# S5 parameters, tables and early weight splits moved to VectorE, complex products over both parts at once, new chain delays

## The chip, the cores and the metric

One NeuronCore of a Trainium2 chip runs the whole program. The metric is the device time of one execution in microseconds (us), the median over several runs. Names of engines in the rows: PE is TensorE's matmul, PEld its weight load, DVE VectorE, ACT ScalarE, POOL GpSimd, SP the engine that issues most DMAs. SBUF is the on-chip memory of 128 partitions, PSUM the banks that matmuls write.

## What is computed

One layer over 1024 prompt positions and 32 new ones, model width 1024. One projection of RMSNorm(x) gives q, k, v, an attention gate ga, the S5 input u and an S5 gate gs, each 512 wide. The attention branch is stick-breaking attention (8 heads of 64). The S5 branch is a complex diagonal state space model with 32 groups of 16 channels and 64 complex states each:

```python
dt = jnp.exp(log_dt)[:, None]; mag = jnp.exp(a_re * dt); ang = a_im * dt
ab_re, ab_im = mag * jnp.cos(ang), mag * jnp.sin(ang)
# f = (ab - 1) / a ; bb = f * b ; bu = ug @ bb
_, _, h_re, h_im = lax.associative_scan(_cmul_combine, (a_s_re, a_s_im, bu_re, bu_im), axis=0)
y = einsum(h_re, c_re) - einsum(h_im, c_im) + d_skip * u
y = gelu(y); y = y * sigmoid(y @ w_glu + b_glu)
out = concat[rmsnorm(att) * silu(ga), rmsnorm(y) * silu(gs)] @ w_out
```

The result is x + out, normed, besides k, v and the last states.

## The kernel before

Every fp32 product runs as three matmuls on a high and a low part of each operand. So weights are split: ScalarE copies w_raw to w_hi, then w_lo = w_raw − w_hi (`w_split`, `w01_split`); x is split the same way (`x_split`: xh on ScalarE, xl on VectorE). `x_sq` squares the rows of x on ScalarE and sums them on VectorE; `x_rs` turns the sum into the factor rsx with matmuls by ones, `rsqrt` on GpSimd and a broadcast by matmul.

`proj_first` (L378 is its matmul) computes the first two projections u0 and u1 while x arrives. Then `proj` (L353) goes through u2, u3, gs0 to gs3, ga0, q0, k0 and v0, each in three pieces of 256, 384 and 416 columns with eight **steps** of three matmuls. After every step `tick` lets the S5 tasks (generators) issue what is due: a task yields a number of steps or the name of something that must be done. So the program order on every engine is fixed when the kernel is built, by the steps at which tasks are started and by the delays in the table WAIT. Each engine then runs its own queue in order.

The S5 work is cut into four groups m of eight channel groups. The parameter chain `params_a` (exp, angle reduction) runs on GpSimd. `angles` makes the rotation table RT by ScalarE's sine, `params_b` to `params_d` the powers PW of the transition and bb. For each m:

- `s_tables` forms three tables by complex products: W (PW times bb, on VectorE), rot (RT far times near, on GpSimd) and V (PW times cv, on GpSimd, for m = 2 on VectorE). A complex product is `cms`: six operations, each over one of the two parts, 512 columns wide.
- `s_mats` transposes W on TensorE (L763), forms Ms (L770, L772) and sends it through DRAM to the tile Tm.
- `u_evac`/`u_raw`, `u_store` and `u_load` move the projection u through DRAM (uj, ud, U).
- `s_states` multiplies U by WT (L873), rotates the result b by rot into E, scans E along time (L891), rotates back into b (named bst in the rows). I call its end S0 to S3.
- `s_out` adds U·Tm (L920) and bst·V (L926), applies GELU, and brings y through DRAM (yd, yj) to y_nat.

After y of group 3, `open_glu` loads the GLU weights, `glu` multiplies (L1033), `ssm_gate` gates with gs on VectorE and GpSimd and ends with `sums`. The attention part, woven with the remaining projections and the output product, follows. `act`, `tt` and `ts` are the helpers that most operations stand under, L96, L99 and L101 to L105.

Of the kernel before, what the change touches and what calls it, by code (L numbers as in the profile page):

```python
# [11 lines left out]
I32 = mybir.dt.int32  # L12
# [15 lines left out]
RSS = 47  # L28
# [40 lines left out]
def hymba_step(ctx, tc, xT, xn, w_in, ln_g, kcT, vc, w_glu, b_glu, w_out, g_att, g_ssm, final_g,  # L69
# [204 lines left out]
    for k in range(1, KT):  # L274
# [91 lines left out]
    def proj_first(evacs, banks):  # L366
# [3 lines left out]
        for c, k in [(0, k) for k in range(LEAD)] + [(c, k - LEAD * c) for k in range(LEAD, KT) for c in range(2)] + \  # L370
# [5 lines left out]
            for n_, (i, f) in enumerate(mms):  # L376
# [7 lines left out]
                if c and k == KT - 1 and f < 2:  # L384
                    w_split(4 + f)
# [1490 lines left out]
```

## Time and profile before

| | |
|---|---|
| runs | 726.07 us median of 3 (725.12 to 727.79) |
| the profiled execution | 723.47 us, span 721.7 us |
| TensorE matmul busy | 638.7 us, 88% of the span |
| VectorE | 505.8 us, 70% |
| GpSimd | 353.4 us, 49% |
| ScalarE | 344.8 us, 48% |
| mean granted TensorE clock | 0.937 of 2.4 GHz |

Busy shares are means over the span, and say little about one stretch; the granted clock is 1.00 or 0.50 at a time. A row of waits names the operation that waited and the one that released it. Matmul durations overlap, so the distance from start to start tells their pace.

### The profile page before, as it was taken

To read this page: it belongs to the slowest core of one execution; us is meant where nothing else is said; L and a number is where in the kernel's file an instruction comes from. 1 tells how busy PE (TensorE), PEld (TensorE's weight loads), DVE (VectorE), ACT (ScalarE), POOL (GpSimd) and SP (SyncE) were. 2 spreads that over 40 slices of the span, in tenths; PEclk is the share of its full clock that TensorE was granted. 3 is DMA by queue.
4 is the path that set the end of the run, shared out by engine and by line. 5 is a ranking of instruction groups with operands and counts; after the bars stand their busy time and mean duration, and the time that the engine had idled before them with its cause. 6 is when DMAs were issued, how large, how long until landed. Compare 5 with 4: busy or idle time off the path is not lost.

```text
span 721.7 us, 10881 instructions
## 1 busy us (share of the span) xinstructions
PE 638.7 (88%) x3834; PEld 574.6 (80%) x3834; DVE 505.8 (70%) x681; ACT 344.8 (48%) x753; POOL 353.4 (49%) x519
## 2 busy tenths in 40 slices
PE   8947987889999998999899999888998789889995
PEld 7947776787898998889889899787878567777883
DVE  5628699988524457678778686867777878695554
ACT  7521221141235464566756557555666647542332
POOL 4875896656222336743344433524135423233785
PEclk8969596989999999999999999999999899999998
DMA  8202522442351136210122112222135465347652
GB/s 306 67 15 67 140 59 73 143 156 71 122 166 60 40 108 216 80 42 23 60 77 75 43 30 82 89 68 94 35 113 165 142 215 165 118 149 214 216 186 94
DMA packets 62645, 79.14 MB, mean 110 GB/s; under 512 B 8864, under 2 KB 47072, under 8 KB 62592
## 3 DMA queue, kind: packets, MB, share of 16 engines
q1 hardware_dynamic: 56256, 66.93, 29.2%
q10 hardware_dynamic: 6336, 11.54, 5.0%
q8 instruction: 30, 0.49, 0.3%
q14 instruction: 23, 0.19, 0.1%
HBM read 51.97 MB, written 26.48 MB: 109 GB/s over the span
## 4 chain that ended last, share of the span: by engine, by line
PE 32%; DVE 19%; ACT 8%; POOL 8%; issue 7%; DMA 3%; ACTq 0%; DVEq 0%; POOLq 0%; SPq 0%
PE pj L353 12%; DVE cb L1169 5%; PE pj L1587 5%; DVE wtl L99 3%; PE z L1033 3%; PE pv L1231 2%; PE tr L1268 2%; PE z L1124 2%; ACT wth L96 2%; DVE kv_out L99 2%; POOL betaL L99 1%; DMA w_raw<-in_w_in 1%; POOL rst L105 1%; ACT cb L96 1%; ACT kA L96 1%
## 5 line engine op out<-in xcount | busy, mean ns | idle before, releaser
L353 PE MATMUL pj<-xh,w_hi 128*128 128x256 f32 (+2 forms) x456 | 160.2, 351 | 0.8 <-DVE kv_out L99 0.8
L353 PE MATMUL pj<-xl,w_hi 128*128 128x256 f32 (+2 forms) x456 | 148.9, 327 | 0.0
L353 PE MATMUL pj<-xh,w_lo 128*128 128x256 f32 (+2 forms) x456 | 148.7, 326 | 0.0
L1169 DVE TENSOR_TENSOR_SCAN cb<-cb 128x896 f32<-128x896 f32 (+8 forms) x66 | 98.9, 1505 | 5.5 <-ACT cb L96 5.4
L99 POOL TENSOR_TENSOR w_lo<-w_raw,w_hi 128x512 fp32r<-128x512 f32 x44 | 68.8, 1564 | 67.8 <-ACT w_hi L96 67.7
L353 PEld LDWEIGHTS pj<-xh,w_hi 128*128 128x128 f32 x456 | 88.8, 195 | 5.8 <-issue 2.6
L353 PEld LDWEIGHTS pj<-xl,w_hi 128*128 128x128 f32 x456 | 88.5, 194 | 1.5
L353 PEld LDWEIGHTS pj<-xh,w_lo 128*128 128x128 f32 x456 | 87.7, 192 | 0.3
L99 POOL TENSOR_TENSOR betaL<-betaL,cb 128x896 f32<-128x896 f32 (+2 forms) x24 | 44.2, 1842 | 70.2 <-DVE cb L1169 36.4
L99 DVE TENSOR_TENSOR wtl<-tr,wth 128x512 fp32r<-128x512 f32 (+2 forms) x86 | 53.5, 625 | 28.2 <-ACT wth L96 27.5
L96 ACT ACTIVATE cb<-z 128x512 f32<-128x512 f32 (+4 forms) x102 | 49.7, 487 | 45.0 <-DVE betaL L99 13.7
L1587 PE MATMUL pj<-xh,S 128*128 128x512 f32 (+3 forms) x212 | 69.2, 406 | 0.5 <-ACT w_raw L96 0.5
L99 POOL TENSOR_TENSOR betaS<-betaS,cb 128x128 f32<-128x128 f32 (+3 forms) x32 | 27.9, 879 | 74.6 <-DVE cb L1169 56.2
L96 ACT ACTIVATE wth<-tr 128x512 fp32r<-128x512 f32 (+2 forms) x86 | 47.3, 551 | 8.8 <-PE tr L1268 6.0
L1231 PE MATMUL pv<-wth,vS 128*128 128x256 f32 x160 | 43.5, 293 | 2.6 <-POOL wth L1208 2.6
L1587 PE MATMUL pj<-xl,S 128*128 128x512 f32 (+3 forms) x112 | 43.8, 393 | 0.7 <-DVE xl L99 0.7
L1268 PE MATMUL tr<-ident,betaL 128*128 128x128 f32 x208 | 33.9, 281 | 11.8 <-DVE wtl L99 9.0
L1587 PEld LDWEIGHTS pj<-xh,S 128*128 128x128 f32 (+2 forms) x212 | 37.9, 192 | 7.5 <-ACT w_raw L96 0.8
L1231 PE MATMUL pv<-wtl,vS 128*128 128x256 f32 x160 | 41.8, 284 | 0.4 <-DVE wtl L99 0.4
L99 DVE TENSOR_TENSOR kv_out<-pj,rsx 128x256 f32<-128x256 f32 (+2 forms) x55 | 28.1, 512 | 17.8 <-PE pj L353 16.8
L1268 PEld LDWEIGHTS tr<-ident,betaL 128*128 128x128 f32 x208 | 25.0, 143 | 17.0 <-DVE wtl L99 10.9
L96 ACT ACTIVATE betaL<-z 128x512 f32<-128x512 f32 (+4 forms) x70 | 35.9, 513 | 0.0
(337 smaller groups left out, 1600.5 us busy)
## 6 DMA issues: line engine op xcount, KB each, us to landing
w_raw<-in_w_in ACTq DMA_DIRECT2D x44, 256.0 KB, 2.6
x<-in_xn SPq DMA_DIRECT2D x8, 512.0 KB, 5.3
yp_d<-x SPq DMA_DIRECT2D x8, 512.0 KB, 5.5
x<-yp_d SPq DMA_DIRECT2D x8, 512.0 KB, 4.5
y_out<-x SPq DMA_DIRECT2D x8, 512.0 KB, 2.9
xr<-in_xT SPq DMA_DIRECT2D x7, 528.0 KB, 7.3
wraw<-in_w_out SPq DMA_DIRECT2D x5, 512.0 KB, 5.1
ud<-uj SPq DMA_DIRECT2D x4, 532.0 KB, 5.8
```

Source lines behind the costliest of these rows:

```text
L96: nc.scalar.activation(out, in_, f, **kw)
L99: (eng or nc.vector).tensor_tensor(out, a, b, op)
L105: (eng or nc.vector).tensor_scalar(out, a, s1, s2, o1, o2)
L353: nc.tensor.matmul(ps[:, :n], a[:, k], b[:, k, t0:t0 + n], start=(k == 0 and f == 0), stop=(k == KT - 1 and f == 2))
L1033: nc.tensor.matmul(ps[:, :n], a[:, k, m * 128:(m + 1) * 128], b[:, k, :n], start=(k == 0 and f == 0), stop=(k == 3 and f == 2))
L1124: nc.tensor.matmul(ps[:, :nn], a, b, start=(i == 0), stop=(i == len(mms) - 1 and mask is None))
L1169: nc.vector.tensor_tensor_scan(cc[:, ::-1], cc[:, ::-1], cc[:, ::-1], 1.0, OP.mult, OP.bypass)
L1231: nc.tensor.matmul(st["ps"][:, 0:256], vs[:, kb, 128 * h:128 * h + 128], w[:, c0:c0 + 256], start=(st["n"] == 0), stop=(st["n"] == 2 * nbl ...
L1268: nc.tensor.transpose(pp[:, c0:c0 + 128], b[:, 128 * kb:128 * kb + 128], ident)
L1587: nc.tensor.matmul(ps[:a.shape[1], :m], a, b_, start=(k == 0 and f == 0), stop=(k == 3 and f == len(mms) - 1))
```

## The change

The parameter chain moves to VectorE, is written with fused operations (a scalar operation and a tensor operation in one), and is placed between the splits of x, by ("p", n) in the list PREP and by `some`; its input pin is loaded from ScalarE's queue. Of the sums of squares the first three go to GpSimd. The low part of the weights of u2 to ga0 is formed on VectorE (WDVE 1 to 8 and the `w_split` in `proj_first`), that of the later ones stays on GpSimd. PW's powers, rot and V come from GpSimd to VectorE, and a complex product is done over both parts at once: `cmw` and `cmr` need wide operations (1024 columns and more) on repeated or negated copies (Pm, Bm, FT, NR) that ScalarE makes. The small copies into rot and fin go from GpSimd to ScalarE. The start steps RSS and PST and the table WAIT have new numbers.

```diff
-RSS = 47
+RSS = 52
...
-PST = 44
+PST = 45
...
-WDVE = 1
-RD = ()
-VD = (2,)
+WDVE = 8
...
-WAIT = {'md': (0, 0, 4, 2), 'Tm': (10, 14, 7, 8), 'ud': (1, 1, 2, 5), ... 'y': (17, 10, 16, 14), 'gate': (10, 10, 10, 11)}
+WAIT = {'md': (0, 0, 6, 0), 'Tm': (11, 14, 6, 0), 'ud': (1, 1, 0, 4), ... 'y': (17, 10, 16, 20), 'gate': (9, 9, 7, 8)}
...
     def x_sq(k):
         act(xr[k], xr[k], AF.Square)
-        if k in SQP:
+        if 0 < k < 4:
             tt(xr[0], xr[0], xr[k], OP.add, nc.gpsimd)
-        elif k > SQD:
-            tt(xr[SQD], xr[SQD], xr[k], OP.add)
+        elif k > 4:
+            tt(xr[4], xr[4], xr[k], OP.add)
+        if k == 7:
+            tt(xr[0], xr[0], xr[4], OP.add)
...
+        stt(t2, t1, -0.693359375, x, OP.mult, OP.add)
...
+        for i in range(6, 0, -1):
+            stt(out, out, 1.0 / math.factorial(i), t2, OP.add, OP.mult)
+            yield
...
+    nc.scalar.dma_start(pin, prm)
...
     x_split(0, first[0])
+    some(7)
     x_split(0, first[1])
+    some(5)
...
-                    w_split(4 + f)
+                    w_split(4 + f, nc.vector)
...
+        def cmw(out, a, s, b, t):
+            n = out.shape[1] // 2
+            tt(t, s, b[:, n:3 * n], OP.mult)
+            yield
+            tt(out, a, b[:, 0:2 * n], OP.mult)
+            yield
+            tt(out, out, t, OP.add)
+            yield
+
+        def cmr(out, a, b, t, conj=False):
+            r = [a[:, i:i + 1].to_broadcast(list(b.shape)) for i in range(2)]
+            tt(t, r[1], b[:, ::-1], OP.mult)
+            yield
+            tt(out, r[0], b, OP.mult)
+            yield
+            for i in range(2):
+                tt(out[:, i], out[:, i], t[:, i], OP.add if conj == (i == 0) else OP.subtract)
+                yield
...
-                   PW[:, 0, :, 1:s + 1], PW[:, 1, :, 1:s + 1], br, bi, t9[:, :, :s], gp)
+                   PW[:, 0, :, 1:s + 1], PW[:, 1, :, 1:s + 1], br, bi, t9[:, :, :s])
...
+            Pm = ss.tile([128, 5, 4, 9], F32, name="Pm")
+            act(Pm[:, 0:2], PW[:, 0:1, g].to_broadcast([128, 2, 4, 9]))
+            act(Pm[:, 2], PW[:, 1, g], scale=-1.0)
...
-            for _ in cms(W[:, 0], W[:, 1], pr, pi, xr_, xi_, t):
+            for _ in cmw(W.rearrange("p r q j c -> p (r q) j c"), two(Pm, 0, slice(0, 8)),
+                         two(Pm, 2, slice(0, 8)), three(Bm), t):
...
-            for _ in cms(ro[0], ro[1], far[0], far[1], near[0], near[1], tv, None if m in RD else gp):
+            for r, f in ((0, FT[:, 2]), (1, RT[:, 1, g, 16:24])):
+                tt(t[:, 4 * r:4 * r + 4], f[..., None].to_broadcast(s4),
+                   RT[:, 1 - r, g, None, 0:16].to_broadcast(s4), OP.mult)
                 yield 1
-            gp.tensor_copy(rot[:, :, :, 128], RT[:, :, g, 24])
+            tt(ro, two(FT, 0), NR.rearrange("p r q k -> p (r q) k")[:, :, None, :].to_broadcast(sh), OP.mult)
+            yield 1
+            tt(ro, ro, t, OP.add)
+            yield 1
+            act(rot[:, :, :, 128], RT[:, :, g, 24])
...
-            for _ in cms(V[:, 0], V[:, 1], pr, pi, xr_, xi_, tv, None if m in VD else gp):
+            for _ in cmw(V.rearrange("p r q j c -> p (r q) j c"), two(Pm, 0, slice(1, 9)),
+                         two(Pm, 3, slice(1, 9)), three(cv), t):
...
-            for _ in cms(E[:, 0, :, n1], E[:, 1, :, n1], rot[:, 0, :, n1], rot[:, 1, :, n1],
-                         b[:, 0, :, n1], b[:, 1, :, n1], t[:, :, n1], None, True):
+            for _ in cmr(E[..., n1], rot[..., n1], b[..., n1], t[..., n1], True):
...
-                gp.tensor_copy(f4[:, i_, :, 4 * m:4 * m + 4], b[:, :, :, n])
+                act(f4[:, i_, :, 4 * m:4 * m + 4], b[:, :, :, n])
```

How the order of instructions moves, at two places. First the opening. Before, GpSimd's queue ends its parameter chain (P) and only then forms w_lo of the third projection:

```order
L99 TENSOR_TENSOR P<-P 128x16
L105 TENSOR_SCALAR P<-P 128x16
L99 TENSOR_TENSOR P<-P 128x16
L628 MEMSET PW 128x16
L629 MEMSET PW 128x16
L103 TENSOR_SCALAR cb<-cb 128x128
L103 TENSOR_SCALAR cv<-cv 128x64
L819 MEMSET uj 128x8
L99 TENSOR_TENSOR w_lo<-w_raw,w_hi 128x512 x2
```

Now the same w_lo stands in VectorE's queue, behind the chain's last operations and the four sums of squares (xr) that VectorE keeps, and ahead of the angle table:

```order
L97 TENSOR_TENSOR P<-P 128x16
L97 TENSOR_TENSOR xr_117<-xr_117,xr_118 128x1056
L97 TENSOR_TENSOR xr_117<-xr_117,xr_119 128x1056
L97 TENSOR_TENSOR xr_117<-xr_117,xr_120 128x1056
L97 TENSOR_TENSOR xr_113<-xr_113,xr_117 128x1056
L603 MEMSET hpi 128x1
L97 TENSOR_TENSOR w_lo<-w_raw,w_hi 128x512 x2
L97 TENSOR_TENSOR ang_v<-kidx,P 128x400
```

The chain and w_lo have changed queues, and VectorE now forms w_lo before it goes on with the angles.

Second, VectorE's queue where the first group's states are rotated (E). Before, the tables rot and V of this stretch are not in it:

```order
L99 TENSOR_TENSOR uj<-pj,rsx 128x8x32
L99 TENSOR_TENSOR W<-PW,bb 128x512
L99 TENSOR_TENSOR tW<-PW,bb 128x512
L99 TENSOR_TENSOR E<-rot,bst 128x4x133
L99 TENSOR_TENSOR W<-W,tW 128x512
L99 TENSOR_TENSOR st_t<-rot,bst 128x4x133
L99 TENSOR_TENSOR E<-E,st_t 128x4x133
```

Now rot and V of the second group stand ahead of the first E, and the products have both parts in one operation:

```order
L97 TENSOR_TENSOR rot<-FT,NR 128x8x128
L97 TENSOR_TENSOR rot<-rot,tW 128x8x128
L97 TENSOR_TENSOR tW<-Pm,cv 128x1024
L97 TENSOR_TENSOR V<-Pm,cv 128x1024
L97 TENSOR_TENSOR uj<-pj,rsx 128x8x32
L97 TENSOR_TENSOR V<-V,tW 128x1024
L97 TENSOR_TENSOR w_lo<-w_raw,w_hi 128x512
L97 TENSOR_TENSOR uj<-pv,rsx 128x8x48
L97 TENSOR_TENSOR st_t<-rot,bst 128x8x133
```

What the scheduler put on GpSimd beside this is now work of the one queue, so E of group 0 comes behind two groups' tables.

On TensorE the steps between projections stay, and the S5 blocks stand at other steps, counted from the first step of u2. The sum by ones moves from step 1 to 6, the first transposes of W0 from 24 to 18, the first states from 31 to 37, the second transposes of W from 42 to 41, the first bst·V products from 55 to 60, those of group 3 from 113 to 111, the first GLU matmul from 157 to 164. From step 240 on the orders agree.

## Rows read from the trace of the kernel before

**Rows 1.** Busy time in four stretches of the program: the S5 stretch (from the last matmul of the two-projection opening to the last S5 product), the way to the GLU, the GLU and what follows up to the first attention tile, the rest. Columns: start and end, length, busy us (and instructions) of PE, PEld, DVE, ACT, POOL, granted TensorE clock, DMA share, GB/s.

```profile
34.30:196.40 162.10, 129.66 (x797) 115.60 (x796) 123.45 (x156) 35.46 (x74) 106.83 (x150) 0.83 0.32 93
196.40:218.80 22.40, 20.98 (x130) 20.38 (x130) 5.83 (x10) 10.91 (x15) 6.10 (x7) 1.00 0.49 155
218.80:287.20 68.40, 65.37 (x400) 64.54 (x400) 36.78 (x51) 35.33 (x66) 29.63 (x21) 1.00 0.31 105
287.20:721.70 434.50, 391.55 (x2351) 344.39 (x2350) 317.59 (x436) 239.88 (x567) 187.76 (x302) 0.97 0.34 108
```

**Rows 2.** TensorE alone in four pieces of the S5 stretch: start and end, length, busy us (matmuls), granted clock, DMA share, GB/s.

```profile
46.20:53.50 7.30, 7.26 (x34) 0.50 0.13 37
...
70.90:87.90 17.00, 15.56 (x76) 0.51 0.66 152
...
114.20:122.00 7.80, 7.80 (x37) 0.51 0.23 70
...
155.00:162.00 7.00, 7.00 (x33) 0.57 0.45 155
```

**Rows 3.** What TensorE waited for from 0 to 230 us: us in total, number of waits, the longest.

```profile
PE z L926 <- DVE bst L99: 12.6, 5, 4.1
PE z L353 <- POOL w_lo L99: 11.5, 1, 11.5
PE tr L763 <- DVE W L99: 6.8, 2, 4.9
```

**Rows 4.** Timeline of GpSimd: start and us, line, operation, output and inputs, shape, count, idle time before it and what ended it.

```profile
43.50 0.26 POOL L99 TENSOR_TENSOR P<-P 128x16 f32<-128x16 f32 x1
...
44.93 2.48 POOL L99 TENSOR_TENSOR w_lo<-w_raw,w_hi 128x512 fp32r<-128x512 f32 x2
...
54.28 0.20 POOL L99 TENSOR_TENSOR rsc<-rsc,rst 128x9 f32<-128x9 f32 x1
...
268.01 2.47 POOL L99 TENSOR_TENSOR y_nat<-y_nat,sgs 128x1056 f32<-128x1056 f32 x1 [2.23 <-DVE y_nat L1061]
```

**Rows 5.** Timeline of VectorE, the opening and the first table, same columns.

```profile
23.91 6.70 DVE L99 TENSOR_TENSOR xr<-xr,xr 128x1056 f32<-128x1056 f32 x5
...
42.70 0.58 DVE L99 TENSOR_TENSOR ang_v<-kidx,P 128x400 f32<-128x400 f32 x1 [12.08 <-POOL P L99]
...
50.26 0.17 DVE L235 COPY rst<-tr 128x8 f32<-128x8 f32 x1 [6.07 <-PE tr L234]
...
52.28 0.37 DVE L105 TENSOR_SCALAR ang_u<-ang_u 128x400 f32<-128x400 f32 x1
...
54.34 0.27 DVE L99 TENSOR_TENSOR PW<-P 128x16 f32<-128x16 f32 x2 [0.38 <-ACT P L96]
...
70.03 0.67 DVE L99 TENSOR_TENSOR W<-W,tW 128x512 f32<-128x512 f32 x1
```

**Rows 6.** VectorE's groups by shape, 60 to 190 us: line, operation, output and inputs, shapes, count, then busy us and mean ns of one, idle time before.

```profile
L891 DVE TENSOR_TENSOR_SCAN E<-dec,E 128x536 f32<-128x536 f32 x8 | 13.4, 1720 | 0.4
L99 DVE TENSOR_TENSOR bst<-E,rot 128x536 f32<-128x536 f32 x8 | 10.4, 1301 | 0.1
...
L99 DVE TENSOR_TENSOR uj<-pv,rsx 128x384 f32<-128x384 f32 x2 | 1.8, 888 | 0.0
L99 DVE TENSOR_TENSOR kv_out<-pv,rsx 128x384 f32<-128x384 f32 x3 | 1.6, 548 | 0.0
...
L99 DVE TENSOR_TENSOR V<-PW,cv 128x512 f32<-128x512 f32 x2 | 1.4, 684 | 0.0
```

**Rows 7.** GpSimd's groups by shape, 60 to 190 us, same columns.

```profile
L99 POOL TENSOR_TENSOR rot<-rot,tV 128x512 f32<-128x512 f32 x8 | 12.7, 1591 | 0.5
```

**Rows 8.** VectorE's groups by shape, 0 to 60 us, same columns.

```profile
L99 DVE TENSOR_TENSOR xr<-xr,xr 128x1056 f32<-128x1056 f32 x7 | 8.8, 1257 | 0.4
...
L99 DVE TENSOR_TENSOR tb<-bm,P 128x256 f32<-128x256 f32 x2 | 0.9, 474 | 0.0
...
L99 DVE TENSOR_TENSOR P<-P 128x16 f32<-128x16 f32 x5 | 0.8, 186 | 0.1
```

**Rows 9.** Timeline of ScalarE, the first split and a DMA issue in its queue, columns as in the timelines above.

```profile
3.71 0.31 ACT L96 ACTIVATE w_hi<-w 128x128 fp32r<-128x128 f32 x1 [1.49 <-DMA w<-in_w_in]
...
46.22 0.34 ACTq L117 DMA_DIRECT2D w_raw<-in_w_in  x1
...
53.84 0.20 ACT L96 ACTIVATE P<-P 128x16 f32<-128x16 f32 x1
```

**Rows 10.** Timeline of VectorE: the first E operation of group 0, then the last bst operation of groups 0 to 3 (112.48 plus 1.66 is S0 at 114.1, and so on).

```profile
89.11 1.06 DVE L99 TENSOR_TENSOR E<-rot,bst 128x532 f32<-128x532 f32 x1 [2.69 <-ACT bst L96]
...
112.48 1.66 DVE L99 TENSOR_TENSOR bst<-bst,st_t 128x536 f32<-128x536 f32 x1
...
137.40 0.72 DVE L99 TENSOR_TENSOR bst<-bst,st_t 128x536 f32<-128x536 f32 x1
...
172.30 0.72 DVE L99 TENSOR_TENSOR bst<-bst,st_t 128x536 f32<-128x536 f32 x1
...
188.71 0.72 DVE L99 TENSOR_TENSOR bst<-bst,st_t 128x536 f32<-128x536 f32 x1
```

**Rows 11.** The chain of waits that ended last, on the way from the last S5 product to the GLU: start us, us, what.

```profile
195.68 0.66 PE z L926 x8
...
218.82 1.57 PE z L1033 x11
```

More of the change, by code (lines that the diff above doesn't have):

```diff
@@ L259, in w01_split, with pv, stt, exp_ @@
         tt(lo_t[c][:, k], w01[c][:, k], hi_t[c][:, k], OP.subtract)
+    P = ss.tile([128, 24, 16], F32, name="P")
+    PW = ss.tile([128, 2, 16, 9], F32, name="PW")
+    n_p = [0]
+    def pv():
+        n_p[0] += 1
+        return P[:, n_p[0] - 1]
+    def stt(out, a, sc, b_, o1, o2):
+        nc.vector.scalar_tensor_tensor(out, a, sc, b_, o1, o2)
+    def exp_(out, x, t1, t2):
+        ts(t1, x, 1.4426950408889634, MAGIC, OP.mult, OP.add)
+        yield
+        ts(t1, t1, MAGIC, -126.0, OP.subtract, OP.max)
+        yield
+        ts(t1, t1, 127.0, None, OP.min)
+        yield
+        stt(t2, t1, -0.693359375, x, OP.mult, OP.add)
+        yield
+        stt(t2, t1, 2.12194440e-4, t2, OP.mult, OP.add)
+        yield
+        ts(out, t2, 1.0 / 5040, None, OP.mult)
+        yield
+        for i in range(6, 0, -1):
+            stt(out, out, 1.0 / math.factorial(i), t2, OP.add, OP.mult)
+            yield
+        ts(t1, t1, 127.0, 8388608.0, OP.add, OP.mult)
+        yield
+        ki = ss.tile([128, 16], I32, name="ki")
+        nc.vector.tensor_copy(ki, t1)
+        yield
+        stt(out, out, 1.0, ki.bitcast(F32), OP.add, OP.mult)
+        yield
@@ new lines, in hymba_step, with params_a @@
+    m8, ph, pl, p8 = pv(), pv(), pv(), pv()
+    are, aim, ldt = pin[:, 0], pin[:, 1], pin[:, 2]
+    dt, mag, ang, fr, fi, w1, w2, w3, phi, den, x1, x2, sn, cs_, ar1 = [pv() for _ in range(15)]
+    def params_a():
+        nc.gpsimd.memset(PW[:, 0, :, 0:1], 1.0)
+        nc.gpsimd.memset(PW[:, 1, :, 0:1], 0.0)
+        yield from exp_(dt, ldt, w1, w2)
+        tt(ang, aim, dt, OP.mult)
+        yield
+        ts(w1, ang, 1.0 / (2 * math.pi), MAGIC, OP.mult, OP.add)
+        yield
+        ts(w1, w1, MAGIC, None, OP.subtract)
+        yield
+        c1 = 6.28125
+        c2 = 0.0019350051879882812
+        c3 = 2 * math.pi - c1 - c2
+        for c in (c1, c2, c3):
+            stt(ang, w1, -c, ang, OP.mult, OP.add)
+            yield
+        ts(phi, ang, 1.0 / (2 * math.pi), 0.5, OP.mult, OP.min)
+        yield
+        ts(phi, phi, -0.5, None, OP.max)
+        yield
+        tt(w3, are, dt, OP.mult)
+        yield
+        yield from exp_(mag, w3, w1, w2)
+        for src in (mag, m8, m8):
+            tt(m8, src, src, OP.mult)
+            yield
+        ts(p8, phi, 8.0, None, OP.mult)
+        yield
+        ts(w1, p8, MAGIC, MAGIC, OP.add, OP.subtract)
+        yield
+        tt(p8, p8, w1, OP.subtract)
+        yield
+        ts(ph, p8, MAGIC / 4096, MAGIC / 4096, OP.add, OP.subtract)
+        yield
+        tt(pl, p8, ph, OP.subtract)
+        yield
@@ L261, in hymba_step, with some @@
+    pa = params_a()
+    def some(n):
+        for _ in range(n):
+            next(pa, None)
     xr = [xp.tile([128, T], F32, name=f"xr{k}") for k in range(KT)]
@@ L300, in hymba_step @@
         elif o[0] == "p":
-            for _ in range(o[1]):
-                next(pa, None)
+            some(o[1])
         else:
@@ L880, in s_states @@
             E = ss.tile([128, 2, 4, NB], F32, name="E")
-            t = ss.tile([128, 4, NB], F32, name="st_t")
+            t = ss.tile([128, 2, 4, NB], F32, name="st_t")
             n1 = slice(1, NB)
@@ L895, in s_states @@
                 yield 1
-            for _ in cms(b[:, 0], b[:, 1], E[:, 0], E[:, 1], rot[:, 0], rot[:, 1], t):
+            for _ in cmr(b, rot, E, t):
                 yield 1
@@ L966, in hymba_step @@
         at_step(PST // 24, PST % 24, spawn, params_d())
-        drain(params_a())
+        done.add("pa")
         at_step(2, 14, open_y1)
```

137 lines of the change are left out of this document (33 added, 104 removed).

## The prediction

> **What bounds the kernel now.** I read the busy time by stage first [rows 1]. TensorE is the busiest engine everywhere, but the S5 stretch from 34.3 to 196.4 us stands out: 162.1 us long, TensorE busy for 129.7 and at 0.83 of its clock, while the 434.5 us after 287.2 run at 0.97. So the S5 stretch has 32.4 us without a matmul, and the pieces of it show the second loss [rows 2]: after each long gap the granted clock is 0.50 to 0.57, the lower of its two levels (1.2 GHz), for a while. Busy time times the missing share gives 7.3×0.50 + 15.6×0.49 + 7.8×0.49 + 7.0×0.43 = 18.1 us in four spells, 4.5 each. TensorE's own work there at full clock is thus 129.7 − 18.1 = 111.6 us, and 50.5 us of the stretch are lost.
>
> The list of TensorE's waits names the gaps [rows 3]: 11.5 us in one piece for w_lo from GpSimd, 12.6 us in five pieces for bst (the finished states of a group), 6.8 us for W. GpSimd is late with w_lo because its queue holds the whole parameter chain, some 60 operations on 16 columns, up to 43.5 us, and w_lo stands behind it at 44.93 [rows 4]. The same chain holds VectorE's angle table back to 42.70, though VectorE has nothing to do from 30.6 on (23.91 + 6.70) [rows 5]. The states are late because VectorE's queue is: between 60 and 190 us an operation on 512 to 536 columns with both inputs in SBUF takes 1.30 us in the mean while GpSimd works on rot, V and w_lo, and 0.68 us where GpSimd had nothing [rows 6]; GpSimd's own take 1.59 [rows 7].
>
> **The change, part by part.** I call a step three projection matmuls; 43 steps lie between the last S5 product and the first GLU matmul, and TensorE is busy 20.98 us there at full clock [rows 1]: 0.49 us a step.
>
> *The opening.* The parameter chain on VectorE is some 46 operations at about 0.19 [rows 8]: 8.6 us. Twelve of them stand between the two halves of the first split and behind the second, fifteen between later splits, the rest behind the last split. Three of the seven sums of squares (1.26 each [rows 8]) go to GpSimd, so VectorE is done at 30.6 + 8.6 − 3.8 − about 2 for the operations that fall into gaps = 33 to 34 us, and w_lo follows at once, near 35 instead of 46.2. TensorE's 11.5 us wait becomes about 1. Bounds: 0 if the chain fits in the gaps altogether, 3 if the three new GpSimd sums (2.47 each at 1056 columns [rows 4]) slow VectorE's splits. The load of pin moves from SP's queue to ScalarE's, ahead of its first table load; ScalarE idles 1.49 us before its first split [rows 9], so I cost it at nothing, and at its 0.34 us issue if that cover were gone. SP is moved past nothing else there.
>
> The rows show that price both ways: 0.68 against 1.30 for two SBUF inputs, and 0.55 for kv_out, whose one input lies in PSUM, in the same stretch [rows 6]. The Trainium skill says the same of the cause (GPSIMD Engine Reference, Specifications): the two engines share their SBUF interfaces, and VectorE instructions with two SBUF inputs contend. By that rule the three new GpSimd sums speak against this change in the opening, for they run beside splits that read two tensors from SBUF, and w_lo would come at 37 to 38.
>
> I take 35, since VectorE still has gaps while those sums run, and keep 3 us of wait as the upper end.
>
> *Sums and the first table.* The row sums now stand at step 6 and the norm's matmuls at step 12. From VectorE's copy to GpSimd's last factor takes 54.5 − 50.3 = 4.2 us [rows 4, 5]; TensorE has 6 steps, 2.9 us, of cover: a new wait of 1 to 2. The angle chain starts at about 36, is held once by the load behind the freed w_raw buffer, and clamps at about 41. From the clamp (52.3) to the first powers (54.6) it took 2.3 us [rows 5], to 43; nine small operations (1.7), eighteen for the powers, which come over from GpSimd (3.4), six for bb at 0.47 (2.8) [rows 8], one w_lo and two uj, 2.2, three wide W operations with 0.4 of casts, 4.2: W0 at 57, against 70.7 now [rows 5]. TensorE reaches the transposes of W0, moved up from step 24 to 18, at about 50 and waits 7. So 8.5 us of waits here.
>
> *The chain on VectorE.* A wide operation (1024 to 1072 columns) I price at 1.25, from the 1056-column sum [rows 8]; the floor is that row, the ceiling, 2.6, twice the 1.30 that a 536-column one took beside GpSimd [rows 6]. Nearest is the first, since GpSimd keeps no tensor work in this stretch. Narrow ones 0.65, a scan 1.72, uj of 384 columns 0.85, kv_out 0.55 [rows 6], in the order of VectorE's queue. From W0 to the first E: 13 wide (rot0, V0, W1, rot1, V1) 16.3, four narrow 2.6, twelve uj 7.8, two w_lo 1.3, dd and Ms 0.6, together 28.5. On to S0: 7 wide 8.8, four narrow 2.6, two scans 3.4, the rest 1.8, together 16.6. To S1: 6 wide, six narrow, two scans, two w_lo and 1.2 of small ones, 17.4. To S2: 15 wide (V2, W3, rot3, V3 among them) 18.8, six narrow 3.9, two scans 3.4, two w_lo 1.3, four kv_out and small ones 2.9, together 30.3. To S3: 4 wide, four narrow, two scans, one w_lo, two kv_out, 12.9. That puts S0 to S3 at 102, 120, 150 and 163, against 114.1, 138.1, 173.0 and 189.4 [rows 10]. rot and V cost nothing on GpSimd any more, and its queue no longer matters.
>
> *Small copies.* About thirteen per group go to ScalarE at 0.2 to 0.3 us [rows 9], some 14 us in all; it is busy 35.5 of 162.1 us there [rows 1], so I cost them at nothing; without that cover each group would start about 3 us later. The fin copies stand ahead of WT and Y in its queue and wait for the states; TensorE has other banks meanwhile. cv and cb loads stay on SP's queue.
>
> *TensorE.* Same matmuls, 111.6 us, less two steps that now come after the last S5 product, 1.0. Waits: 1 for w_lo, 8.5 for the sums and W0, 6 for W2 (it is ready near 96, and TensorE comes to its transposes near 90), 1.5 for S1, 2 for the rest: 19. Slow clock after two of them and a bit: 10. Sum 139.6, so the last S5 product ends at 173.9 instead of 196.4: 22.5 us earlier. Then the GLU stands 52 steps on instead of 43, that is 25.5 us, while the way through Y, yd, yj and the GLU's weights takes 218.8 − 196.4 = 22.4 [rows 1, 11]: covered now, and the GLU begins at 199.4, 19.4 us earlier. Seven steps fewer remain after it, 3.4 us, but the gate chain of VectorE and GpSimd begins with the GLU's end too; I count half. Everything after 287.2 [rows 1] is only shifted. **Sum: −21 us.** The profiled execution, 723.5 us (1.8 around the 721.7 span), lies 2.6 below the runs' median of 726.1; on the median this is **705**.
>
> **Rivals.**
> - *VectorE alone sets the pace.* If the waits for W2 and S1 vanish and the clock holds, S3 at 163 with 7 us of products ends the stretch at 170; with the 25.5 us to the GLU and the full 3.4 after it this is −27: 699. For it: ready times on VectorE are estimates from above. Against: the 7 us gap at W0 is about what cost a slow spell before [rows 2].
> - *Gain given back.* The GpSimd sums hold VectorE's splits, by the 1.30 row against 0.68 [rows 6]: the wait for w_lo is 3 instead of 1, W0 comes 3 later, one more slow spell costs 4.5 [rows 2], and the gate chain keeps its 68.4 us [rows 1], so that the 1.7 fall away. 21 − 2 − 3 − 4.5 − 1.7 leaves −10: 716. For it: all three are waits of one queue. Against: VectorE's gaps in the opening. This is also what the rule named above, of the Trainium skill's GPSIMD Engine Reference, would make of the opening.
> - *VectorE becomes the bound, slower.* 45 wide operations lie between W0 and S3. At 1.85 us each S3 falls back to 189; at 2.4, about two contended narrow ones, it is 25 us later than now: 751. For it: one engine now carries what two did. Against: nothing on GpSimd is left to contend with, and the 1056-column row.
> - *No change.* w_lo waits on VectorE behind sums and parameters as long as on GpSimd. Against: VectorE's free time from 30.6 to 42.7 [rows 5].
>
> **How the numbers follow.** My forecast has 0.58, the faster rival 0.20, the partial one 0.13, the slower one 0.04, no change 0.05. A difference under 0.5% is what a measurement of this kernel can't tell from none. Forecast, faster and partial rival lie beyond that: faster 0.91, same 0.05, slower 0.04. The range from 692 to 718 holds these three with the bounds of the opening (0 to 3), of W0's wait and of the prices on VectorE; it leaves out the slower rival and no change.
>
> **What would show it.** Right: TensorE's wait for w_lo under 3 us; no mean over 0.8 us left among VectorE's 532-column operations; GpSimd almost idle from 60 to 170; W0 near 57, S3 near 163; the GLU near 200; the stretch from the GLU to the first attention tile 65 to 68 us; the clock low after the waits for W0 and W2. Wrong: wide operations at 1.8 us or more; ScalarE's copies as releasers of VectorE for more than a microsecond each; a TensorE wait of over 12 us at W0; or an attention part that differs by more than 3 us.

## The result and the profile after

The changed kernel takes 706.2 us (median of four runs on the chip of the kernel before, which had 726.9). One of the four, 770.6, was disturbed; it is in that median, and the ratio leaves it out (the other three have the median 705.0). The ratio is 0.971, with a 95% interval from 0.967 to 0.975: faster, 1.2 us above the forecast of 705. The profiled execution took 704.95, its span 703.1.

By stage, columns as in [rows 1], with the boundaries at the same places: the opening's end, the last S5 product, the first GLU matmul (before, one GLU matmul runs at 217.56 ahead of the boundary, and the next waits until 218.82), the row-sum matmuls ahead of the first attention tile.

```profile
38.96:176.40 137.44, 120.57 (x790) 106.23 (x789) 118.20 (x183) 42.82 (x125) 12.54 (x29) 0.91 0.36 107
176.40:201.90 25.50, 25.50 (x157) 25.39 (x158) 9.42 (x14) 11.79 (x16) 4.26 (x5) 1.00 0.50 162
201.90:263.40 61.50, 61.14 (x380) 60.55 (x379) 34.59 (x48) 34.18 (x64) 25.80 (x18) 1.00 0.30 101
263.40:703.10 439.70, 394.47 (x2352) 348.23 (x2350) 315.13 (x437) 240.17 (x567) 188.74 (x304) 0.96 0.34 108
```

Against [rows 1]: the S5 stretch went from 162.1 to 137.4 and starts 4.7 us later, the way to the GLU from 22.4 to 25.5 (TensorE busy throughout), the GLU part from 68.4 to 61.5, and the rest, whose order the change leaves as it was, from 434.5 to 439.7. So 24.7 + 6.9 were won and 4.7 + 3.1 + 5.2 given back; 18.6 remain. GpSimd's work in the S5 stretch fell from 106.8 to 12.5 us.

What TensorE waited for in the S5 stretch (us in total, number, longest), against [rows 3]:

```profile
PE tr L912 <- DMA U<-ud: 6.5, 1, 6.5
PE tr L802 <- DVE W L97: 4.5, 2, 3.6
PE z L439 <- DVE w_lo L97: 2.4, 1, 2.4
PE z L964 <- DVE bst L97: 2.2, 1, 2.2
PE tr L243 <- POOL rsc L97: 1.3, 1, 1.3
```

These five are the whole 16.9 us without a matmul in the stretch (137.44 − 120.57). The 11.5 for w_lo are 2.4, the 12.6 for bst 2.2. A 6.5 us wait for the load of U is new.

VectorE by shape, 45 to 170 us, against [rows 6] (busy us, mean ns of one, idle before):

```profile
L929 DVE TENSOR_TENSOR_SCAN E<-dec,E 128x536 f32<-128x536 f32 x8 | 10.0, 1269 | 0.4
L97 DVE TENSOR_TENSOR w_lo<-w_raw,w_hi 128x512 fp32r<-128x512 f32 x10 | 6.9, 692 | 2.1 <-ACT w_hi L94 2.0
L97 DVE TENSOR_TENSOR bst<-bst,st_t 128x536 f32<-128x536 f32 x8 | 5.4, 715 | 0.1
L97 DVE TENSOR_TENSOR bst<-rot,E 128x1072 f32<-128x1072 f32 x4 | 5.1, 1269 | 0.0
...
L97 DVE TENSOR_TENSOR tW<-Pm,Bm 128x1024 f32<-128x1024 f32 x4 | 4.9, 1222 | 3.4 <-ACT Bm L94 3.4
```

The third of these rows as it was before, 60 to 190 us:

```profile
L99 DVE TENSOR_TENSOR bst<-bst,st_t 128x536 f32<-128x536 f32 x8 | 9.1, 1140 | 0.2
```

That 536-column operation takes 715 ns where it took 1140, and a scan 1269 where it took 1720. The product of E and rot, 1301 for each half before [rows 6], is now one wide operation of 1269; wide ones take 1.22 to 1.29 us. The last line also shows VectorE idle for 3.4 us behind a ScalarE copy (Bm).

VectorE's last bst operation of groups 0 to 3, against [rows 10] (each pair ends at S0 = 107.2, S1 = 123.0, S2 = 155.4, S3 = 167.8; before 114.1, 138.1, 173.0, 189.4):

```profile
105.81 1.35 DVE L97 TENSOR_TENSOR bst<-bst,st_t 128x536 f32<-128x536 f32 x2
...
121.70 1.34 DVE L97 TENSOR_TENSOR bst<-bst,st_t 128x536 f32<-128x536 f32 x2
...
154.05 1.34 DVE L97 TENSOR_TENSOR bst<-bst,st_t 128x536 f32<-128x536 f32 x2
...
166.48 1.33 DVE L97 TENSOR_TENSOR bst<-bst,st_t 128x536 f32<-128x536 f32 x2
```

In the opening the forecast missed. VectorE (columns as in [rows 5]):

```profile
16.28 0.42 DVE L97 TENSOR_TENSOR w_lo<-w,w_hi 128x256 fp32r<-128x256 f32 x1
...
18.34 2.71 DVE L97 TENSOR_TENSOR w_lo<-w,w_hi 128x256 fp32r<-128x256 f32 x1
20.97 2.87 DVE L271 SCALAR_TENSOR_TENSOR P<-P 128x16 f32<-128x16 f32 x3
23.88 2.44 DVE L103 TENSOR_SCALAR P<-P 128x16 f32<-128x16 f32 x1
...
35.73 5.34 DVE L97 TENSOR_TENSOR xr<-xr,xr 128x1056 f32<-128x1056 f32 x4
41.00 0.69 DVE L97 TENSOR_TENSOR w_lo<-w_raw,w_hi 128x512 fp32r<-128x512 f32 x1
...
59.70 1.23 DVE L97 TENSOR_TENSOR W<-W,tW 128x1024 f32<-128x1024 f32 x1
```

and GpSimd at the same time:

```profile
17.80 5.59 POOL L97 TENSOR_TENSOR xr<-xr,xr 128x1056 f32<-128x1056 f32 x2 [16.91 <-ACT xr L94]
23.85 2.43 POOL L97 TENSOR_TENSOR xr<-xr,xr 128x1056 f32<-128x1056 f32 x1 [0.46 <-ACT xr L94]
```

A split of 256 columns takes 0.42 us at 16.28 and 2.71 at 18.34, and an operation on 16 columns, 0.17 us elsewhere, takes 2.44 at 23.88: it ends at 26.32, and GpSimd's sum at 26.28. By these ends VectorE was not slowed; it stood still until GpSimd's instruction was over. So it came to its own sums (35.73) and the first w_lo (41.00) late.

### The profile page after: what moved, and what is told of

Its sections match the earlier page's. It is cut to its first block, busy times and chain, and to the rows that moved or that the text cites. A ratio compares the mean times of both kernels' runs of the same rounds, so it can differ in the third digit from the quotient of the medians.

```text
span 703.1 us, 10847 instructions
## 1 busy us (share of the span) xinstructions
PE 634.0 (90%) x3834; PEld 570.9 (81%) x3834; DVE 508.2 (72%) x751; ACT 352.7 (50%) x805; POOL 241.6 (34%) x369
## 4 chain that ended last, share of the span: by engine, by line
PE 28%; DVE 11%; ACT 5%; issue 4%; POOL 1%; DMA 1%; DVEq 0%; ACTq 0%; POOLq 0%
PE pj L1625 8%; PE pj L439 7%; DVE cb L1207 4%; PE z L1625 4%; DVE wtl L97 3%; PE pv L1269 3%; PE tr L1306 2%; PE z L1162 2%; ACT wth L94 2%; DVE kv_out L97 1%; DVE betaL L97 1%; PE z L1358 1%; ACT cb L94 1%; DMA kc_raw<-in_vc 1%; DVE attT L97 1%
## 5 line engine op out<-in xcount | busy, mean ns | idle before, releaser
L1207 DVE TENSOR_TENSOR_SCAN cb<-cb 128x896 f32<-128x896 f32 (+8 forms) x66 | 96.6, 1471 | 4.7 <-ACT cb L94 4.6
L97 POOL TENSOR_TENSOR betaL<-betaL,cb 128x896 f32<-128x896 f32 (+2 forms) x24 | 42.2, 1760 | 73.7 <-DVE cb L1207 54.4
L97 POOL TENSOR_TENSOR w_lo<-w_raw,w_hi 128x512 fp32r<-128x512 f32 x30 | 49.2, 1640 | 41.7 <-ACT w_hi L94 41.7
L94 ACT ACTIVATE wth<-tr 128x512 fp32r<-128x512 f32 (+2 forms) x86 | 47.2, 550 | 11.5 <-PE tr L1306 9.7
L1306 PEld LDWEIGHTS tr<-ident,betaL 128*128 128x128 f32 x208 | 25.9, 147 | 17.8 <-DVE wtl L97 10.9
```

The costliest lines, as they stand in the source:

```text
L94: nc.scalar.activation(out, in_, f, **kw)
L97: (eng or nc.vector).tensor_tensor(out, a, b, op)
L1207: nc.vector.tensor_tensor_scan(cc[:, ::-1], cc[:, ::-1], cc[:, ::-1], 1.0, OP.mult, OP.bypass)
L1306: nc.tensor.transpose(pp[:, c0:c0 + 128], b[:, 128 * kb:128 * kb + 128], ident)
```

## Experiments

Each was timed against the kernel before on the same chip. The changed kernel (706.2, ratio 0.971) was not run again beside them, so a difference to it compares two ratios. Those of experiments 1, 2 and 7 (4 to 5 us) have intervals that overlap with its 0.967 to 0.975; there the rows carry the argument. The gains of 1 and 7 together are clear of it (e12 in experiment 8: 0.958 to 0.966).

**1. Who holds VectorE in the opening: e1_sums_dve.** In the changed kernel:

```diff
-            tt(xr[0], xr[0], xr[k], OP.add, nc.gpsimd)
+            tt(xr[0], xr[0], xr[k], OP.add)
```

> The changed kernel with the first three sums of squares back on VectorE, at the places in its queue where the change has them. In the changed kernel's trace VectorE's instructions between 18.3 and 26.3 us end when GpSimd's sums end: a split of 256 columns takes 2.71 us (0.42 elsewhere), three operations on 16 columns 2.87 (0.6), one 2.44 (0.17), 6.8 us in all. Theory 1, GpSimd's sum holds VectorE for its whole length: the 6.8 us go, 3 x 1.26 = 3.8 come, so the first w_lo of the projections comes at 38 instead of 41.0, TensorE ends the opening 2 to 3 us earlier than 38.96, W0 is done near 58 (60.9), S3 near 165 (167.8), and the time is 703 to 705. Theory 2, the two engines only share a little and the stretched rows are waits of another kind: VectorE gets 3.8 us more to do, w_lo at 42 to 45, the time 707 to 710.

Measured: 702.1, ratio 0.966 (0.962 to 0.970), 4 us faster. The opening ends at 32.0 instead of 38.96, w_lo comes at 36.5, W0 is done at 56.9, S3 at 163.6. On VectorE the three operations that took 2.87 us are back at 0.59:

```profile
18.51 0.59 DVE L271 SCALAR_TENSOR_TENSOR P<-P 128x16 f32<-128x16 f32 x3
...
36.49 0.69 DVE L97 TENSOR_TENSOR w_lo<-w_raw,w_hi 128x512 fp32r<-128x512 f32 x1
```

Theory 1 holds, with a time just below its 703 to 705; the opening gained more than it said (7 us), and TensorE gave 2.4 of that back waiting longer for w_lo (4.8).

**2. The same price in the S5 stretch: e2_wlo_gp.** In the changed kernel:

```diff
-  w_split(2 * ci + 2 + i, nc.vector if ci < WDVE else None)
+  w_split(2 * ci + 2 + i)
```

> The changed kernel with the weight splits of the S5 stretch (ten w_lo of 512 columns between 45 and 170 us) on GpSimd instead of VectorE; the two of the opening stay on VectorE. Theory 1, a GpSimd tensor operation holds VectorE while it runs: VectorE loses 10 x 0.69 = 6.9 us of its own and is held 10 x 1.3 to 2.4 = 13 to 24 us, so S3 comes 6 to 15 us later than 167.8, rows of VectorE at 1.9 us and more show up among those of 512 to 536 columns, and the time is 709 to 716. Theory 2, an engine that carries less is done sooner: S3 at 161 to 163, the 2.2 us wait of TensorE for S2 gone, the time 701 to 704.

Measured: 710.3, ratio 0.978 (0.973 to 0.983), 4 us slower. Time and direction are theory 1's; S3, at 171.7, is 3.9 us late instead of 6 to 15. VectorE's long rows, and GpSimd's at the same times:

```profile
84.22 2.29 DVE L97 TENSOR_TENSOR rot<-FT,NR 128x1024 f32<-128x1024 f32 x1
86.55 2.18 DVE L97 TENSOR_TENSOR rot<-rot,tW 128x1024 f32<-128x1024 f32 x1
...
105.56 2.34 DVE L97 TENSOR_TENSOR bst<-rot,E 128x1072 f32<-128x1072 f32 x1
```

```profile
83.73 1.70 POOL L97 TENSOR_TENSOR w_lo<-w_raw,w_hi 128x512 fp32r<-128x512 f32 x1
85.50 2.14 POOL L97 TENSOR_TENSOR w_lo<-w_raw,w_hi 128x512 fp32r<-128x512 f32 x1
...
105.21 1.55 POOL L97 TENSOR_TENSOR w_lo<-w_raw,w_hi 128x512 fp32r<-128x512 f32 x1 [4.32 <-ACT w_hi L94]
```

Each GpSimd split lengthens one VectorE operation by 0.9 to 1.1 us (2.29 for 1.22, 2.34 for 1.27). Nine of them ahead of S3 make 9 us. VectorE's own splits start 0.6 us apart (41.00 and 41.60 in the changed kernel), so the nine that are gone from there free 5.4. It also idles 0.8 us more behind Bm (4.2 for 3.4) and 1.1 less behind w_hi; that leaves 3.3 of the 3.9. I had let every split hold VectorE for as long as its stretched row says (up to 2.3); but GpSimd's row too contains waiting, since it stands still while VectorE's instruction runs (1.27 alone, 1.84 in the mean).

**3. Tables alone: e5_tables_only.** In the kernel before:

```diff
-RD = ()
-VD = (2,)
+RD = (0, 1, 2, 3)
+VD = (0, 1, 2, 3)
```

> The kernel before with one part of the change alone: the complex products of all rot and V tables on VectorE, in the old form (six operations on 512 columns, 42 of them moved), opening, delays and all else as before. Theory 1, GpSimd's tensor operations held VectorE: its rows of 512 to 536 columns fall from 1.3 to 0.7 us and the scans from 1.72 to 1.27, some 50 us less, against 42 x 0.69 = 29 more, so S3 comes at 165 to 178 instead of 189.4, the last S5 product at 178 to 188 instead of 196.4, and the time is 708 to 719. Theory 2, the load only moves: VectorE has 29 us more to do, S3 comes after 200, and the time is 730 to 745.

Measured: 718.2, ratio 0.987 (0.981 to 0.994). S3 at 182.7, the last S5 product near 189.5; the bst rows of 1301 ns fall to 840:

```profile
L891 DVE TENSOR_TENSOR_SCAN E<-dec,E 128x536 f32<-128x536 f32 x8 | 12.2, 1537 | 0.4
L99 DVE TENSOR_TENSOR bst<-E,rot 128x536 f32<-128x536 f32 x8 | 6.7, 840 | 0.1
L99 DVE TENSOR_TENSOR bst<-bst,st_t 128x536 f32<-128x536 f32 x8 | 5.7, 710 | 0.1
```

Theory 1: VectorE took over 42 operations, some 29 us, and was done 6.7 us sooner. The positions lie 2 to 5 us behind its range; GpSimd keeps the powers and w_lo here, and the scans are still at 1537, which fits that but was not tried apart.

**4. Early splits alone: e10_split_only.** In the kernel before:

```diff
-                    w_split(4 + f)
+                    w_split(4 + f, nc.vector)
```

> The kernel before with the first two w_lo splits of the projections on VectorE (idle there from 30.6 us) instead of behind the parameter chain on GpSimd; the chain itself, the tables and all else as before. Theory 1, a wait removed alone comes back at the next late thing: the 11.5 us wait for w_lo becomes 0 to 3, but W0 stays near 70.7, TensorE waits there 10 to 15 us instead of 4.9, the last S5 product stays within 3 us of 196.4, and the time is 723 to 728. Theory 2, it is on the path by itself: the last S5 product 8 to 10 us earlier, 715 to 719.

Measured: 721.0, ratio 0.991 (0.988 to 0.994), between the two. The wait for w_lo is 7.6 instead of 11.5, that for W 8.4 (6.8), that for bst 16.0 (12.6): of 3.9 us taken away, 5.0 come back at the next two places. Why 7.6 is left, on VectorE:

```profile
32.28 0.69 DVE L99 TENSOR_TENSOR w_lo<-w_raw,w_hi 128x512 fp32r<-128x512 f32 x1 [1.17 <-ACT w_hi L96]
...
43.80 0.57 DVE L99 TENSOR_TENSOR ang_v<-kidx,P 128x400 f32<-128x400 f32 x1 [10.82 <-POOL P L99]
44.29 0.68 DVE L99 TENSOR_TENSOR w_lo<-w_raw,w_hi 128x512 fp32r<-128x512 f32 x1
```

The first split is done at 33.0, but the second stands behind ang_v, which waits 10.8 us for GpSimd's parameter chain. In this order of the queue the early split gains little as long as the chain is late: the two edits belong together. Where the median's 6 us came from stays open: the profiled execution was the slowest of the ten (726.2 of 717.9 to 726.2).

**5. The delays: e8_old_delays.** The changed kernel with WAIT, RSS (47) and PST (44) of the kernel before.

> The changed kernel with the delays, the step of the row sums and the step of the angle chain of the kernel before. Theory 1, the delays set the order in which the waiting instructions stand in ScalarE's and TensorE's queues, and the old ones put waits for VectorE ahead of copies that TensorE needs, as the one changed delay of the U load did for 15 us: TensorE has waits of 5 us and more for ScalarE's bst or WT, the last S5 product comes at 183 to 195, the time is 712 to 722. Theory 2, the delays are fine tuning: the last S5 product within 3 us of 176.4, the time 705 to 709.

Measured: 719.9, ratio 0.991 (0.988 to 0.994): two thirds of the change's 20 us are gone. The time is theory 1's, with waits of 5.8 us behind a ScalarE copy at the states' matmuls (Pm, not the bst or WT that it named) and 7.9 for W; the last product, at 180.6, lies below its range. The GLU starts at 202.0 as in the changed kernel, but the old order puts fewer projection matmuls ahead of it: 457 instead of 400 are left from there to the first attention tile, which comes at 285.5 instead of 265.6. In that part TensorE also idles for 5.0 us and its granted clock is 0.94 instead of 1.00.

**6. One delay: e4_u_early and e9_u_early_fin.** In the table WAIT the delay of the first load of U (8 steps to 2), then also the fin copies off ScalarE:

```diff
-WAIT = {... 'ul': (8, 3, 1, 1), ...}
+WAIT = {... 'ul': (2, 3, 1, 1), ...}
```

```diff
-  act(f4[:, i_, :, 4 * m:4 * m + 4], b[:, :, :, n])
+  gp.tensor_copy(f4[:, i_, :, 4 * m:4 * m + 4], b[:, :, :, n])
```

> The changed kernel with the first load of U issued 2 steps behind its store (as before) instead of 8, so that it stands ahead of the store of Ms in SyncE's queue. TensorE waits 6.5 us for this load at 75.2 to 81.7. Theory 1, VectorE sets the pace from W0 on: the wait shrinks to 1 or less, but S0 to S3 stay within 2 us of 107.1, 123.0, 155.3 and 167.8, a wait for bst of 3 to 6 us takes its place, and the last S5 product stays within 2 us of 176.4: 704 to 707. Theory 2, the wait is on the path: the last S5 product 4 to 6.5 us earlier, 700 to 702.

Measured: 720.9, ratio 0.992 (0.989 to 0.995), 15 us slower; both theories fell. The wait for U went (1.4), but TensorE waits 17.7 us for ScalarE's bst copies, and S3 comes at 177.0. ScalarE:

```profile
74.62 0.63 ACT L94 ACTIVATE Pm<-PW 128x72 f32<-128x72 f32 x4 [8.40 <-DVE V L97]
...
76.50 0.64 ACT L94 ACTIVATE bst<-tr 128x266 f32<-128x266 f32 x2
...
104.39 0.32 ACT L94 ACTIVATE fin<-bst 128x8 f32<-128x8 f32 x2 [9.23 <-DVE bst L97]
104.61 0.66 ACT L94 ACTIVATE bst<-tr 128x266 f32<-128x266 f32 x2
106.25 0.60 ACT L94 ACTIVATE WT<-tr 128x512 f32<-128x512 f32 x1 [0.98 <-PE tr L802]
```

With U there earlier, TensorE is now ready for group 0's bst copies while they stand in ScalarE's queue behind Pm, which waits for V (8.4 us), and two of group 1's come to stand behind fin, which waits for S0 (9.2). In the changed kernel all four of group 1 run at 96.6 to 100.4, ahead of fin at 107.2.

> The kernel with the earlier load of U (720.9), with the copies of the final states (fin) back on GpSimd instead of ScalarE. With the early load ScalarE waits 9.2 us at 95.2 to 104.4 in the fin copy of group 0 for VectorE's last bst operation; behind it stand two bst copies of group 1, for which TensorE waits 7.9 us. Theory 1, that copy is what turned the earlier load into a loss: this wait goes, and with it the waits for bst that follow, the last S5 product 6 to 12 us earlier than in that kernel, the time 707 to 714. Theory 2, VectorE is late for group 1 anyway, and TensorE waits as long at the next place: 717 to 722.

Measured: 709.4, ratio 0.975 (0.969 to 0.980). The time is theory 1's: 11.5 us back with eight small copies moved. The waits for bst went from 17.7 us to 1.6, but those for W rose from 2.1 to 8.6, and the last S5 product is only 4 us earlier (180.1), less than the 6 to 12 given. The rest came behind the GLU's start (205.5 for 209.4), where the same matmuls keep TensorE busy for 7 us less: its granted clock is 1.00 up to the first attention tile instead of 0.95, and 0.98 behind it instead of 0.97. Why the clock differs there was not shown, so not all of the 11.5 is shown to be the copies' doing.

**7. The attention part: e3_gate_dve.** In the changed kernel:

```diff
-                tt(yv, yv, sg, OP.mult, gp)
+                tt(yv, yv, sg, OP.mult, gp if m < 3 else None)
```

> The changed kernel with the last of the four gate products (1056 columns, 2.47 us) on VectorE instead of GpSimd. In the changed kernel it runs on GpSimd until 267.9, the sums of the norm are there at 265.5, the norm's chain on GpSimd ends at 271.3 and ScalarE's first sigmoid of the attention starts at 270.78; TensorE's lead over the kernel before falls there from 23.8 us (first attention tile) to 19.6. Theory 1, that product delays the norm and with it the first sigmoid: the sigmoid starts near 268, the stretch from the first attention tile to the end is 433 to 435 instead of 437.4, and the time 2 to 4 us shorter, 702 to 704. Theory 2, the lost microseconds are slow-clock spells of TensorE or the memory that the attention's tiles wait for: the stretch stays at 436 to 438, the time 705 to 707.

Measured: 701.0, ratio 0.965 (0.961 to 0.970), 5 us faster; the first attention tile at 265.6 as in the changed kernel, from there 433.1 instead of 437.5. First GpSimd in the changed kernel, where the gate product (2.5 us) stands ahead of the norm's chain, then ScalarE's first sigmoid in the changed kernel, then the same in this run:

```profile
265.44 2.47 POOL L97 TENSOR_TENSOR y_nat<-y_nat,sgs 128x1056 f32<-128x1056 f32 x1
268.00 0.21 POOL L103 TENSOR_SCALAR rst<-rsc 128x9 f32<-128x9 f32 x1
268.29 1.84 POOL L97 TENSOR_TENSOR rsS<-rst,mhalf 128x9 f32<-128x9 f32 x1
```

```profile
270.78 0.60 ACT L94 ACTIVATE cb<-z 128x512 f32<-128x512 f32 x1 [3.01 <-POOL rst L97]
```

```profile
267.84 0.60 ACT L94 ACTIVATE cb<-z 128x512 f32<-128x512 f32 x1 [0.44 <-POOL rsS L97]
```

Theory 1, with a time just below its 702 to 704: the sigmoid starts 2.9 us earlier, and TensorE's clock in the 13.4 us after 263.4 is granted at 0.87 instead of 0.78 (1.00 before). Theory 2 was half right: part of the loss is slow clock, which shrank with that wait.

**8. Both edits, and two more on top: e7_sums_gate, e12_fin_gp, e11_late58, e13_late52.** e7 has the edits of experiments 1 and 7; e12 adds the fin copies on GpSimd; e11 and e13 move the last four sums (x_add: sums 5, 6 and 7 into xr[4], then that into xr[0]) behind the first two w_lo, e11 with RSS = 58 and RSW = 66:

```diff
                     if f:
                         w_load(6)
+                        x_add()
```

> The changed kernel with both of the single edits that made it faster: the three sums of squares on VectorE (4 us alone) and the last gate product on VectorE (5 us alone). Theory 1, they act in different places (before 60 us, after 260 us) and add: first attention tile near 262.5, from there to the end 433 to 434, the time 696 to 699. Theory 2, the second only undoes a collision that the first moves away too: 700 to 703.

Measured: 698.6, ratio 0.961 (0.954 to 0.968): the gains add within the intervals (4 and 5 us alone), 7.6 us under the changed kernel. No run here has a lower median; e12's is level with it.

> The kernel with both single edits (698.6), with the copies of the final states (fin) on GpSimd instead of ScalarE, where they wait 21.7 us in the changed kernel. Theory 1, with the change's own delays nothing that TensorE or VectorE needs stands behind these copies: S3 within 2 us of 163.6, the last S5 product within 2 us of 172.9, the time 697 to 701. Theory 2, they hold ScalarE's other copies as they do with the earlier load of U: S2 and S3 come 3 us earlier and the time is 693 to 696.

Measured: 698.7, ratio 0.962 (0.958 to 0.966): with the change's own delays moving the fin copies changes nothing that shows, as theory 1 had it.

> The kernel with both single edits (698.6), in which VectorE also does its last four sums of squares behind the first two w_lo splits instead of ahead of them, and the row sums and the norm's matmuls stand 6 steps later. TensorE's wait for w_lo there is 3.3 us, that for W0 3.6. Theory 1, VectorE's work up to W0 is the same whatever its order, so TensorE only waits at another place: w_lo wait under 1, but 5 to 7 at W0 or at the row sums, S3 within 2 us of 163.6, the time 697 to 701. Theory 2, the wait was lost time: 694 to 696.

Measured: 713.0, ratio 0.983 (0.978 to 0.988), 14 us slower; neither theory. On VectorE and TensorE:

```profile
32.04 0.68 DVE L97 TENSOR_TENSOR w_lo<-w_raw,w_hi 128x512 fp32r<-128x512 f32 x1
...
50.40 0.16 DVE L236 COPY rst<-tr 128x8 f32<-128x8 f32 x1
```

```profile
38.43 2.10 PE L235 MATMUL tr<-ones,xr 128*128 128x1 f32 x18 [0.67 <-DVE xr L97]
54.96 1.11 PE L804 MATMUL tr<-ident,W 128*128 128x128 f32 x4 [9.45 <-DVE W L97]
58.10 1.22 PE L244 MATMUL tr<-ident,rsc 128*128 128x128 f32 x4 [2.03 <-POOL rsc L97]
```

The row sums are ready at 40.5, but their copy on VectorE now stands behind the powers and runs at 50.40, and TensorE's norm matmuls stand behind the transposes of W0 (54.96).

> The kernel with both single edits (698.6) and VectorE's last four sums of squares behind the first two w_lo splits, with the row sums at their old step. With the row sums 6 steps later (713.0) VectorE's small copy of them stood at 50.4 us, behind the whole chain of powers, and TensorE's matmuls of the norm behind the transposes of W0; so that kernel did not tell whether the 3.3 us wait for w_lo is worth anything. Theory 1, TensorE then waits for the row sums as long as it waited for w_lo (they are done 38.4, it comes there at 35.5), W0 stays at 56.8, S3 within 2 us of 163.6: 697 to 701. Theory 2, the wait was lost time: 694 to 696.

Measured: 700.9, ratio 0.963 (0.959 to 0.967): theory 1 by the rows: the wait for w_lo is gone, and a wait of 2.9 us for the row sums stands in its place. The six runs lie between 696.4 and 704.2, so the time alone would not show 2 us either way.

## Why the prediction was right, point by point

The sum was right, and so was its centre: the tables' work left GpSimd, VectorE's operations fell to their lone prices, and the S5 stretch shortened by what its queue gave. Of the single terms several were off, and that they cancelled to 2.5 us is luck. How the gain divides among the parts was not forecast: the tables alone give 9 us (experiment 3), the early splits 6 (4), and without the new delays two thirds are gone (5). What the wide form is worth by itself was not run; by the rows one operation of 1024 columns takes 1.22 us where two of 512 take 2 × 0.69.

- **Opening (failed).** "VectorE still has gaps while those sums run", w_lo near 35: it came at 41.0, and the opening itself ended 4.7 us later than before. The gaps don't help, because a GpSimd sum held VectorE nearly for its whole length (2.27 us of 2.43 at 23.88; experiments 1, 2). The Trainium skill says so outright (SBUF — State Buffer, SBUF: two separate sides): between a GpSimd operation and a VectorE operation with two SBUF inputs (or in a two-port mode) the one that starts first has the shared ports for its whole instruction, and the other blocks. The prediction cited a weaker sentence on contention and took 37 to 38 from it; the rows at 18.34 to 26.32 agree with the strong one (the operation at 23.88 reads one tensor, so it falls under the bracket; its mode stands in no row). The term was −10.5 in TensorE's wait; −4.4 came (9.1 less wait, 4.7 later start). That later start was put at nothing without a reason: the forecast kept TensorE's opening end at 34.3, though VectorE's splits of x feed it, and the last of these ended at 31.98 instead of 23.99.
- **Row sums:** a new wait of 1 to 2; 1.3 measured.
- **W0 at 57, wait 7:** 60.9, wait 3.6. VectorE was late by what the opening lost, TensorE as well.
- **Prices on VectorE:** wide 1.25 (measured 1.22 to 1.29), narrow 0.65 (0.69 to 0.72), uj 0.85 (0.88). The scan at 1.72 was too dear: its row [rows 6] came from a time when GpSimd held VectorE; alone it takes 1.27, 3.6 us less over eight scans.
- **S0 to S3 at 102, 120, 150, 163:** 107.2, 123.0, 155.4, 167.8, 3 to 5 late; W0 was 3.9 late.
- **Waits of TensorE, 19:** 16.9, but not the ones listed. W2's 6 did not come (0.9 did); 6.5 for the load of U did, which no step of mine had. Its issue (74.04) stands in SyncE's queue behind the store of Ms (73.62). Removing it by its delay alone made things worse (experiment 6), so that it is lost time was not shown.
- **Slow clock, 10:** 120.57 × 0.09 = 10.9, but not at the places named. The granted clock is 0.50 from 60 to 65, from 80 to 85 and from 155 to 160 us, behind the waits for W0, U and S2, and 0.72 from 40 to 45, where the wait for w_lo lies; from 90 to 115, where W2 is transposed, it is 1.00.
- **Work at full clock, 110.6:** 120.57 − 10.9 = 109.7. The 18.1 us of slow clock before were too few: the four pieces of [rows 2] leave some out, and the stretch's own clock [rows 1] gives 129.66 × 0.17 = 22.0.
- **"Other banks meanwhile"** for the fin copies: right with these delays (e12), wrong with one delay changed (e4, e9: two of the bst copies stood behind fin for 9.2 us).
- **Small copies at nothing (failed at one place):** VectorE waits 3.4 us for Bm, whose copy stands in ScalarE's queue behind Y, which waits for TensorE's product. It is a sign that the prediction named for wrong (over a microsecond behind ScalarE's copies). It lies between S1 and S2, and S2 is what TensorE waits 2.2 us for ahead of the slow clock at 155. No run took it away. On VectorE and ScalarE:

```profile
130.92 1.23 DVE L97 TENSOR_TENSOR tW<-Pm,Bm 128x1024 f32<-128x1024 f32 x1 [3.38 <-ACT Bm L94]
129.87 0.68 ACT L94 ACTIVATE Y<-z 128x266 f32<-128x266 f32 x2 [2.98 <-PE z L964]
```

- **Last S5 product 173.9, GLU 199.4:** 176.4 and 201.9; the cover of 25.5 us is exact, without a wait.
- **After the GLU, −1.7; attention only shifted (failed):** the two parts were won and lost apart: −6.9 up to the attention, +5.2 in it, together the −1.7, which is luck. In the first (65 to 68 us named, 61.5 came), TensorE's work fell by 4.2 us (20 matmuls fewer) and its idle time from 3.0 to 0.4, so the gate chain took nothing back there. The second is the sign named for wrong, over 3 us in the attention part. The gate chain came closer to the norm's: GpSimd's last product ended 2.2 us before the row sums arrived before, and 2.4 after them now (experiment 7).

Of the rivals, the partial one was right about the opening: its wait of 3 for w_lo and its W0 3 us later are near the 2.4 and 3.9 that came. Its further slow-clock spell did not come, so 716 was not reached. Measured against 702.5 for the profiled execution, the terms are +4.7 (opening), −2.2 (S5 stretch 137.4 for 139.6), −5.2 (GLU part), +5.2 (attention), together 2.5: 704.95.

## What to carry to other kernels

Ask of each GpSimd tensor operation what VectorE does at that moment: beside VectorE operations on SBUF it cost VectorE nearly its own length here (0.9 to 1.1 us for one of 1.27), so moving 0.69 us of work away from a busy VectorE lost time. A price from a row that was measured beside such work is no price for the time after. In a program whose queues are in written order, a delay chooses what stands behind what; change it, and read which copy now waits ahead of the one that the engine on the critical path needs.

## What was not expected of the hardware

- A VectorE operation on 16 columns took 2.44 us (0.17 alone) beside a GpSimd sum of 1056 columns; the stretched time is inside its row, not in the idle column.
- The hold goes both ways: ten GpSimd splits of 512 columns took 1.84 us in the mean beside a busy VectorE, the shortest 1.27 (experiment 2).
- A VectorE operation whose one input lies in PSUM did not stretch: in the kernel before, kv_out of 384 columns ran from 170.69 us for 544 ns, wholly inside a GpSimd product (170.16 to 171.69); after, without such products, it takes 542 in the mean. Of the three such kv_out in [rows 6] only this one ran beside a table of GpSimd.
